# Sums of gate and up weights for a seven-product block multiplication: built in DRAM by accumulating DMAs, or added by VectorE in SBUF

## The chip, the cores and the metric

The kernel runs on one core of one Trainium2 chip. The metric is device time in microseconds, the median of several executions. For the kernel before, three runs gave 2494.14, 2497.13 and 2497.49 us, a median of 2497.13 us.

## What is computed

The reference is one inference step of a two-layer decoder: 1024 prompt tokens and 8 sample tokens with a model width of 1024. Layer 0 mixes by a gated linear recurrence, layer 1 by stick-breaking attention; both add attention over 256 memory tokens and end in a SwiGLU feed-forward network:

```
def swiglu(h, w_gu, w_down):
    gate, up = jnp.split(h @ w_gu, 2, axis=-1)
    return (jax.nn.silu(gate) * up) @ w_down
```

For one layer `w_gu` is 1024 x 5632 (2816 gate columns, then 2816 up columns) and `w_down` is 2816 x 1024, all float32. The change concerns this network of layer 1 for the second half of the tokens, which is the last large stage of the program.

## The kernel before

**Tokens and precision.** The tokens are worked in two groups: group 0 holds 512 prompt tokens, group 1 the other 512 prompt tokens and the 8 sample tokens, so 520 columns. Activations lie with the model dimension on the 128 partitions. Every float32 matrix product is made as three matmuls: each operand is split into a rounded high part and the rest, and high x high, high x low and low x high are accumulated. For weights ScalarE makes the high part (a cast, L260 or L542) and VectorE the low part (a subtraction, L261 or L543).

**The feed-forward network** has 22 blocks of 128 gate columns with their 128 up columns. They are grouped by PARTS (L613) into parts of 5, 5, 4, 4 and 4 blocks. In a part, the blocks give `mids` (silu(gate) x up), and then `w_down` for the same rows is multiplied and added up in `R` (L660 to L676).

**The last network** (class ffn_w, L615, group 1, layer 1) makes blocks 0 to 3 plainly (gate_up_q, L499) and blocks 4 to 21, 18 blocks, by a block multiplication with seven products in place of eight (gate_up_w, L524). The gate weights are cut into upper rows a11 and lower rows a12 (512 rows each), the up weights into a21 and a22, and the tokens into two halves of 260 columns. Seven products `product(ps, 0..6)` (L546) of 12 matmuls each use the weights a11, a21+a22, a11+a21+a22, a12, a11+a21, a11+a21+a22+a12, a22 and matching sums of the activations (sums_w, L326, done once). Between them stand small operations: ScalarE copies one accumulator with a sign change into another ahead of products 2 and 5 (L559, L562), takes silu (L565, L574) and a copy (L568); VectorE adds and subtracts (L570, L572) and multiplies (L575, L576); and the block's result is split for the next product (L281 by ScalarE, L282 by VectorE).

**Where the sums of weights come from.** weight_sums (L588) runs much earlier, in the layer-1 network of group 0 (f1, L1500 to L1503). For each part it makes four DRAM tensors `wsum` of 512 rows by plain and accumulating DMAs that GpSimd issues (L606, L608), eight per part, 40 in all. Each is tied to the progress of f1: ScalarE copies one element of the newest f1 result (`tok`, L602), GpSimd copies that (`mark`, L603), and the DMA is issued behind the mark. In the last network `weight(j)` (L535) then loads each of the seven 512 x 128 weights of a block by one 256 KB DMA on SyncE's queue (L537), three from `w_gu` and four from `wsum`.

**Buffers.** The raw weights come from `wraw` (5 tiles of 128 x 512) and, after the first part, every second one from half a tile of `apool` (8 tiles, of which 4 are kept as `hT`, residual rows for the end, so that 4 remain). `raws` (L630) chooses. The split weights come from `wspl` (5 tiles) and, after the first part, three of eight from `cpool` (4 tiles, one kept by the rows of the sample tokens); `spl` (L624) chooses. `w_down` weights use `wraw` and `wspl` too. `cpool` also carries `yo`, the finished rows of group 0 on their way to DRAM (store_y, L1445, stores L1456): these and the turned residual rows (token_rows, L476, L484) are woven with the first two parts of ffn_w (L1525).

**Order.** Each engine runs its instructions in a fixed order, laid out when the program is built, by a scheduler that sees data dependences and free buffers. All loads of weights and most stores stand in one order on SyncE's queue.

Of the kernel before, what the change touches and what calls it, by code (L numbers as in the profile page):

```python
# [2 lines left out]

# [15 lines left out]
P = 128  # L19
# [5 lines left out]
def tile_decoder(  # L25
# [46 lines left out]
    def nm(s):  # L72
        uid[0] += 1
        return f"{s}_{uid[0]}"
# [12 lines left out]
    def Q(i):  # L87
        return single[0].tile([P, 512], F32, tag=f"q{i}", name=nm("q"))
# [32 lines left out]
    def small(shape, dt=F32, tag="sm", bufs=None):  # L121
        return spool.tile(shape, dt, tag=tag, name=nm(tag), bufs=bufs)
# [105 lines left out]
    def chain(*gens):  # L228
        for g_ in gens:
            yield from g_  # L230
# [92 lines left out]
            out.append(x)  # L323
            yield

    def sums_w(xs, ops):  # L326

        n, h = NG[1], PW[1]  # L330
        for k in range(4):
            x0, x1 = xs[k], xs[k + 4]
            y = YT()
            if k % 2 == 0:
                z, u = YT(), YT()
            o = (k % 2) * h

            def full(x, c):
                t = B()
                nc.vector.tensor_add(t[:, :h], x[:, 0, c : c + h].bitcast(F32), x[:, 1, c : c + h].bitcast(F32))  # L340
# [13 lines left out]
            yield  # L354

    def YT():
        return xpool.tile([P, 2, NG[1]], F32R, tag="x0", name=nm("y"))

    def wo_tiles(g):
# [161 lines left out]
        split_to((mt[:, 0, :n], mt[:, 1, :n]), sg[:, :n])  # L521
        return mt, last

    def gate_up_w(l, f, ops, spl, raws):  # L524

        h, n = PW[1], NG[1]
        part, o = part_of(f)
        gate, up = f * P, DFF + f * P
        src = [
            (w_gu[l][0:512, gate : gate + P], 0), (sums[l][part][0][:, o : o + P], 4), (sums[l][part][1][:, o : o + P], 5),  # L530
            (w_gu[l][512:D, gate : gate + P], 1), (sums[l][part][2][:, o : o + P], 6), (sums[l][part][3][:, o : o + P], 2),
            (w_gu[l][512:D, up : up + P], 3),
        ]

        def weight(j):  # L535
            r = raws()
            nc.sync.dma_start(r, src[j][0].rearrange("(k p) m -> p k m", p=P))  # L537
            return r.rearrange("p k m -> p (k m)")

        def split(src):  # L540
            w = spl()
            nc.scalar.copy(w[:, 0, :], src)  # L542
            nc.vector.tensor_sub(w[:, 1, :], src, w[:, 0, :].bitcast(F32))  # L543
            return w

        def product(ps, j, first=False):  # L546
            w = split(weight(j))
            i = src[j][1]
            for k in range(4):
                x = ops[k][i]  # L550
                for wi, (wj, xi) in enumerate(((0, 0), (0, 1), (1, 0))):
                    nc.tensor.matmul(  # L552
                        ps[:, :h], w[:, wj, k * P : (k + 1) * P], x[:, xi, :],
                        start=(first and k == 0 and wi == 0), stop=(k == 3 and wi == 2), skip_group_check=True,
                    )

        pa, pb, pc, pd = (Q(i) for i in range(4))
        product(pa, 0, True)
        nc.scalar.activation(pb[:, :h], pa[:, :h], AF.Copy, scale=-1.0)  # L559
# [5 lines left out]
        nc.scalar.activation(sg[:, :h], pa[:, :h], AF.Silu)  # L565
        product(pb, 4)
        dt = T()
        nc.scalar.copy(dt[:, h:n], pd[:, :h])  # L568
        gt = T()
        nc.vector.tensor_add(gt[:, h:n], dt[:, h:n], pb[:, :h])  # L570
        product(pc, 5)
        nc.vector.tensor_sub(gt[:, :h], pc[:, :h], dt[:, h:n])  # L572
        product(pb, 6)
        nc.scalar.activation(sg[:, h:n], gt[:, :h], AF.Silu)  # L574
        nc.vector.tensor_mul(sg[:, :h], sg[:, :h], pb[:, :h])  # L575
        nc.vector.tensor_mul(sg[:, h:n], sg[:, h:n], gt[:, h:n])  # L576
        mt = M(F32R)
        split_to((mt[:, 0, :n], mt[:, 1, :n]), sg[:, :n])
        return mt

    sums = {}

    def part_of(f):
        for i, (f0, nf) in enumerate(PARTS):
            if f0 <= f < f0 + nf:
                return i, (f - f0) * P

    def weight_sums(l, parts, after):  # L588

        for i in parts:  # L590
            f0, nf = PARTS[i]
            w = nf * P
            s1, s2, s3, s4 = (tc.dram_tile([512, w], F32, name=nm("wsum")) for _ in range(4))
            sums.setdefault(l, {})[i] = (s1, s2, s3, s4)
            a11, a12 = (w_gu[l][r : r + 512, f0 * P : f0 * P + w] for r in (0, 512))
            a21, a22 = (w_gu[l][r : r + 512, DFF + f0 * P : DFF + f0 * P + w] for r in (0, 512))
            for d, a, add in (
                (s3, a11, False), (s1, a21, False), (s3, a21, True), (s1, a22, True),
                (s2, s3, False), (s2, a22, True), (s4, s2, False), (s4, a12, True),
            ):  # L600
                tok = small([P, 1], tag="rr")
                nc.scalar.copy(tok, after())  # L602
                mark = nc.gpsimd.tensor_copy(small([P, 1], tag="mk", bufs=1), tok)  # L603
                with tc.issue_after(mark.ins):
                    if add:
                        nc.gpsimd.dma_start(d, a, accum_op=ALU.add)  # L606
                    else:
                        nc.gpsimd.dma_start(d, a, max_dma_last_dim=4 * w)  # L608
                yield

    htok = []

# [2 lines left out]
    class ffn_w:  # L615


        def __init__(self, l, x, plain):
            self.g, self.l, self.x, self.ops, self.plain, self.n, self.r, self.pi = 1, l, x, [], plain, 0, 0, 0
            self.R = self.acc = None  # L620
            self.half = []
            self.sums = sums_w(x, self.ops)

        def spl(self):  # L624
            self.n += 1
# [2 lines left out]
            return wspl.tile([P, 2, 512], F32R, tag="ws", name=nm("ws"))  # L628

        def raws(self):  # L630
            self.r += 1
            if self.pi and self.r % 2:
                if not self.half:
                    t = apool.tile([P, 2, 4, P], F32, tag="a", name=nm("w"))
                    self.half = [t[:, 0], t[:, 1]]
                return self.half.pop(0)
            return wraw.tile([P, 4, P], F32, tag="w", name=nm("w"))

        def part(self, pi):
            l, n, h = self.l, NG[1], PW[1]  # L640
# [3 lines left out]
            for j in range(nf):  # L644
                self.pi = pi
                if f0 + j < self.plain:
                    mt, ins = gate_up_q(l, f0 + j, self.x)
                    mids.append(mt)
                    with tc.issue_after(ins.ins):
                        for _ in range((1, 2, 1, 0)[j]):  # L650
                            next(self.sums, None)
                else:
                    mids.append(gate_up_w(l, f0 + j, self.ops, self.spl, self.raws))
                yield
            if pi == 0:
                self.R = R_one()
# [31 lines left out]
    class ffn:  # L688
# [4 lines left out]
        def part(self, pi):  # L693
# [5 lines left out]
            for j in range(nf):  # L699
                pg = proj(g, w_gu[l], 0, ND, (f0 + j) * P, self.xt)  # L700
                sg = silu(None, pg, g)
                pu = proj(g, w_gu[l], 0, ND, DFF + (f0 + j) * P, self.xt)
                nc.vector.tensor_mul(sv(sg, g), sv(sg, g), pv(pu, g))  # L703
                mt = M(F32R)
                split_to((mt[:, 0, :n], mt[:, 1, :n]), sg[:, :n])
                mids.append(mt)
                self.now = sg[:, 0:1]
                yield
            if pi == 0:
                self.R = R_one()  # L710
# [2 lines left out]
            for m in range(ND):  # L713
                ps = proj(g, w_down[l], f0, nf, m * P, mids)
                evac_raw(g, self.R, ps, m, self.acc, pi == 0, last)
                self.now = self.R[m][:, 0:1]
# [842 lines left out]
```

## Time and profile before

| | |
|---|---|
| median of three runs | 2497.13 us |
| profiled execution, its own time | 2499.1 us |
| span of the profiled execution | 2497.4 us |
| TensorE matmul / weight load busy | 2462.8 / 2169.9 us |
| VectorE / ScalarE / GpSimd busy | 1571.8 / 1183.0 / 98.3 us |
| DMA traffic | 358.21 MB, of this 54.53 MB from GpSimd's queue |
| f1 with weight_sums (first to last DMA of weight_sums) | 1036.7 to 1457.0 us |
| ffn_w: plain blocks, block 4, first w_down | from 2115.3, 2164.1, 2176.8 us |
| ffn_w: blocks 5-9, 10-13, 14-17, 18-21 | from 2209.3, 2288.4, 2351.8, 2415.2 us |
| last w_down ends, rows stored | 2481.2, to 2497.4 us |

Times in the profile are counted from the start of the span. A row of grouped instructions gives the line, the engine, the operation, the tile that is written and the tiles that are read, the number of instructions, the busy time and the mean duration of one, and then the idle time of the engine just before them with what ended it. "PE" is TensorE, "PEld" its weight load, "DVE" VectorE, "ACT" ScalarE, "POOL" GpSimd, "SPq" SyncE's DMA queue.

### The profile page before, as it was taken

To read this page: it belongs to the slowest core of one execution; us is meant where nothing else is said; L and a number is where in the kernel's file an instruction comes from. 1 tells how busy PE (TensorE), PEld (TensorE's weight loads), DVE (VectorE), ACT (ScalarE), POOL (GpSimd) and SP (SyncE) were. 2 spreads that over 40 slices of the span, in tenths; PEclk is the share of its full clock that TensorE was granted. 3 is DMA by queue.
4 is the path that set the end of the run, shared out by engine and by line. 5 is a ranking of instruction groups with operands and counts; after the bars stand their busy time and mean duration, and the time that the engine had idled before them with its cause. 6 is when DMAs were issued, how large, how long until landed. Compare 5 with 4: busy or idle time off the path is not lost.

```text
span 2497.4 us, 40764 instructions
## 1 busy us (share of the span) xinstructions
PE 2462.8 (99%) x15565; PEld 2169.9 (87%) x15565; DVE 1571.8 (63%) x2756; ACT 1183.0 (47%) x2277; POOL 98.3 (4%) x139
## 2 busy tenths in 40 slices
PE   8999999999999999999999999999999999999998
PEld 6888988877877897999999989877787797999997
DVE  5766556655765585655544575777577648755655
ACT  5446543243433454555433454555444445564444
POOL 1000000000000000010111100022000000000000
PEclk9999999999999999999999999999999999999999
DMA  5352252233643447586678976544454234365542
GB/s 186 114 165 68 72 156 81 60 110 116 184 124 98 129 138 227 156 195 177 173 191 215 234 193 196 160 142 138 121 149 130 85 115 122 121 192 145 151 137 69
DMA packets 496110, 358.21 MB, mean 143 GB/s; under 512 B 19110, under 2 KB 443635, under 8 KB 495915
## 3 DMA queue, kind: packets, MB, share of 16 engines
q1 hardware_dynamic: 477354, 301.08, 40.5%
q0 software_dynamic: 18560, 54.53, 9.1%
q8 instruction: 122, 2.00, 0.3%
q14 instruction: 74, 0.60, 0.1%
HBM read 325.73 MB, written 75.94 MB: 161 GB/s over the span
## 4 chain that ended last, share of the span: by engine, by line
PE 88%; DVE 5%; DMA 3%; ACT 2%; issue 2%; POOL 0%; SPq 0%; DVEq 0%; ACTq 0%; POOLq 0%
PE mm L274 59%; PE q L552 7%; PE q L667 5%; PE s L1180 2%; PE q L510 2%; PE mm L1048 2%; PE s L903 1%; PE s L862 1%; PE mm L812 1%; DMA b<-qd 1%; PE mm L839 1%; DVE ws L261 1%; PE ns L957 1%; PE s L1336 1%; DMA c<-in_cache_sb_v,pidx 1%
## 5 line engine op out<-in xcount | busy, mean ns | idle before, releaser
L274 PE MATMUL mm<-x,ws 128*128 128x260 f32 (+1 forms) x7776 | 1332.9, 330 | 0.0
L274 PEld LDWEIGHTS mm<-x,ws 128*128 128x128 f32 x7776 | 1148.3, 188 | 151.5 <-issue 12.0
L260 ACT CAST ws<-w 128x512 fp32r<-128x512 f32 x712 | 420.2, 591 | 763.2 <-PE mm L274 620.2
L261 DVE TENSOR_TENSOR ws<-w,ws 128x512 fp32r<-128x512 f32 x712 | 462.5, 653 | 286.8 <-ACT ws L260 278.3
L274 PE MATMUL mm<-m,ws 128*128 128x512 f32 (+1 forms) x2112 | 393.5, 343 | 0.1
L274 PEld LDWEIGHTS mm<-m,ws 128*128 128x128 f32 x2112 | 324.4, 189 | 49.9 <-issue 2.6
L667 PE MATMUL q<-m,ws 128*128 128x260 f32 x1056 | 128.8, 283 | 0.0
L667 PEld LDWEIGHTS q<-m,ws 128*128 128x128 f32 x1056 | 127.2, 188 | 0.4 <-ACT hT L485 0.2
L543 DVE TENSOR_TENSOR ws<-w,ws 128x512 fp32r<-128x512 f32 x126 | 86.6, 691 | 61.5 <-ACT ws L542 59.3
L552 PE MATMUL q<-y,ws 128*128 128x260 f32 x864 | 112.9, 283 | 0.0
L542 ACT CAST ws<-w 128x512 fp32r<-128x512 f32 x126 | 78.0, 621 | 69.6 <-PE q L667 27.4
L552 PEld LDWEIGHTS q<-y,ws 128*128 128x128 f32 x864 | 107.6, 189 | 0.0
L291 DVE TENSOR_SCALAR t<-mm 128x512 f32<-128x512 f32 (+1 forms) x82 | 56.7, 692 | 79.6 <-PE mm L274 79.6
L447 DVE TENSOR_TENSOR r<-r,mm 128x512 f32<-128x512 f32 (+1 forms) x96 | 66.0, 688 | 61.1 <-PE mm L274 60.3
L703 DVE TENSOR_TENSOR t<-t,mm 128x512 f32<-128x512 f32 (+1 forms) x66 | 45.5, 690 | 74.2 <-PE mm L274 73.9
L295 DVE TENSOR_TENSOR t<-t,t 128x512 f32<-128x512 f32 (+1 forms) x66 | 45.8, 694 | 70.6 <-ACT t L294 70.6
L552 PE MATMUL q<-x,ws 128*128 128x260 f32 x648 | 86.3, 282 | 0.0
L552 PEld LDWEIGHTS q<-x,ws 128*128 128x128 f32 x648 | 81.3, 188 | 0.0
L314 DVE TENSOR_TENSOR st<-st,n 128x512 f32<-128x512 f32 (+1 forms) x98 | 67.1, 691 | 8.8 <-ACT n L313 7.0
L281 ACT CAST m<-t 128x512 fp32r<-128x512 f32 (+1 forms) x88 | 54.9, 624 | 18.1 <-DVE t L703 8.9
L282 DVE TENSOR_TENSOR m<-t,m 128x512 fp32r<-128x512 f32 (+1 forms) x88 | 61.0, 693 | 2.6 <-ACT m L281 1.4
L984 POOL DMA_INDIRECT c<-in_cache_sb_k,pidx x16 | 16.4, 1026 | 1170.5 <-ACT n L313 958.6
(339 smaller groups left out, 2557.9 us busy)
## 6 DMA issues: line engine op xcount, KB each, us to landing
w<-in_w_gu SPq DMA_DIRECT2D x334, 256.0 KB, 3.4
w<-in_w_down SPq DMA_DIRECT2D x160, 256.0 KB, 3.5
w<-in_w_in_a SPq DMA_DIRECT2D x80, 256.0 KB, 3.0
wsum<-in_w_gu POOLq DMA_DIRECT2D x18, 1024.0 KB, 9.5
w<-wsum SPq DMA_DIRECT2D x72, 256.0 KB, 3.8
w<-in_w_o SPq DMA_DIRECT2D x64, 256.0 KB, 2.8
wsum<-in_w_gu POOLq DMA_DIRECT2D x12, 1280.0 KB, 10.7
w<-in_w_mem_kv SPq DMA_DIRECT2D x32, 256.0 KB, 3.2
```

The costliest lines, as they stand in the source:

```text
L260: nc.scalar.copy(ws[:, 0, :n, :], raw[:, :n, :])
L261: nc.vector.tensor_sub(ws[:, 1, :n, :], raw[:, :n, :], ws[:, 0, :n, :].bitcast(F32))
L274: nc.tensor.matmul(ps[:, a, : PW[g]], wt, xt[k][:, xi, o : o + PW[g]], start=(k == 0 and wi == 0), stop=(k == nk - 1 and wi == 2),)
L281: nc.scalar.copy(dst[0], src)
L282: nc.vector.tensor_sub(dst[1], src, dst[0].bitcast(F32))
L291: nc.vector.tensor_scalar(sv(x, g), pv(ps, g), -44.0, None, op0=ALU.max)
L314: nc.vector.tensor_add(acc[:, :n], acc[:, :n], t[:, :n])
L447: nc.vector.tensor_add(dst, dst, pv(ps, g))
L542: nc.scalar.copy(w[:, 0, :], src)
L543: nc.vector.tensor_sub(w[:, 1, :], src, w[:, 0, :].bitcast(F32))
L552: nc.tensor.matmul(ps[:, :h], w[:, wj, k * P : (k + 1) * P], x[:, xi, :], start=(first and k == 0 and wi == 0), stop=(k == 3 and wi == 2), ...
L667: nc.tensor.matmul(pp[a][:, :h], wt, mids[k][:, xi, a * h : (a + 1) * h], start=(k == 0 and wi == 0), stop=(k == nf - 1 and wi == 2),)
```

## The change

weight_sums, part_of and the `tok` and `mark` copies go; f1's last three parts run alone. gate_up_w now takes its weights from sums_here: it loads the gate column of the block whole (1024 rows x 128, one DMA of 512 KB) and the up column likewise, into two tiles, and makes the four sums by four VectorE additions (a21+a22; a11+a21; that + a22; that + a12) into `wraw` tiles. a11, a12 and a22 are read where they lie. The two column tiles come from `cpool` for block 4 (first part) and from `apool` afterwards. The seven products, their split and the operations between them are unchanged. Built, the changed program has 72 more VectorE instructions, 40 fewer on ScalarE, 80 fewer on GpSimd and 90 fewer on SyncE, and as many matmuls as before.

```
-    def gate_up_w(l, f, ops, spl, raws):
+    def sums_here(l, f, raws, outs):
+        cols = []
+        for m0 in (f * P, DFF + f * P):
+            r = raws()
+            nc.sync.dma_start(
+                r.rearrange("p a (k m) -> p (a k) m", m=P), w_gu[l][:, m0 : m0 + P].rearrange("(k p) m -> p k m", p=P)
+            )
+            cols.append(r)
+        (a11, a12), (a21, a22) = ((r[:, 0, :], r[:, 1, :]) for r in cols)
+        kept = {}
+
+        def add(a, b):
+            t = outs()
+            nc.vector.tensor_add(t, a, b)
+            return t
+
+        def weight(j):
+            if j == 1:
+                return add(a21, a22)
+            if j == 2:
+                kept[3] = add(a11, a21)
+                kept[2] = add(kept[3], a22)
+                return kept[2]
+            if j == 4:
+                return kept[3]
+            if j == 5:
+                return add(kept[2], a12)
+            return (a11, None, None, a12, None, None, a22)[j]
+
+        return weight
+
+    def gate_up_w(weight, ops, spl, quads):
...
-        def weight(j):
-            r = raws()
-            nc.sync.dma_start(r, src[j][0].rearrange("(k p) m -> p k m", p=P))
-            return r.rearrange("p k m -> p (k m)")
...
-    def weight_sums(l, parts, after):
...
         def raws(self):
-            self.r += 1
-            if self.pi and self.r % 2:
-                if not self.half:
-                    t = apool.tile([P, 2, 4, P], F32, tag="a", name=nm("w"))
-                    self.half = [t[:, 0], t[:, 1]]
-                return self.half.pop(0)
-            return wraw.tile([P, 4, P], F32, tag="w", name=nm("w"))
+            if self.pi:
+                return apool.tile([P, 2, 512], F32, tag="a", name=nm("w"))
+            return C()
...
-    ws = weight_sums(1, range(5), lambda: f1.now)
-    weave((chain(b0.sb(), b0.mem()), 24), (chain(f1.part(0), f1.part(1)), 18), (islice(ws, 16), 17))
-    weave((chain(f1.part(2), f1.part(3), f1.part(4)), 24), (ws, 24))
+    weave((chain(b0.sb(), b0.mem()), 24), (chain(f1.part(0), f1.part(1)), 18))
+    drain(f1.part(2), f1.part(3), f1.part(4))
```

More of the change, by code (lines that the diff above doesn't have):

```diff
@@ L1 @@
 from contextlib import ExitStack
-from itertools import islice
 import concourse.bass as bass
@@ L522, in gate_up_q @@
         return mt, last
-    def gate_up_w(l, f, ops, spl, raws):
-        h, n = PW[1], NG[1]
[L527 to L533, printed above, removed]
-        def weight(j):
-            r = raws()
-            nc.sync.dma_start(r, src[j][0].rearrange("(k p) m -> p k m", p=P))
-            return r.rearrange("p k m -> p (k m)")
+    def sums_here(l, f, raws, outs):
[26 more added lines that the diff above has]
+    def gate_up_w(weight, ops, spl, quads):
+        h, n = PW[1], NG[1]
+        src = (0, 4, 5, 1, 6, 2, 3)
         def split(src):
@@ L555, in product @@
                     )
-        pa, pb, pc, pd = (Q(i) for i in range(4))
+        pa, pb, pc, pd = quads()
         product(pa, 0, True)
@@ L578, in gate_up_w @@
         split_to((mt[:, 0, :n], mt[:, 1, :n]), sg[:, :n])
[L579 to L586, printed above, removed]
-    def weight_sums(l, parts, after):
[L590 to L609, printed above, removed]
+        return mt, last
     htok = []
@@ L652, in part @@
                 else:
-                    mids.append(gate_up_w(l, f0 + j, self.ops, self.spl, self.raws))
+                    mids.append(gate_up_w(
+                        sums_here(l, f0 + j, self.raws, lambda: wraw.tile([P, 512], F32, tag="w", name=nm("w"))),
+                        self.ops, self.spl, lambda: [Q(i) for i in range(4)]
+                    )[0])
                 yield
```

15 lines of the change are left out of this document (6 added, 9 removed).

## Prediction

> **What bounds the kernel now.** I read the page's busy times first, then TensorE's waits in the two stages that the change touches, then the chain of waits of the last stage.
>
> ```profile
> PE 2462.8 (99%) x15565; PEld 2169.9 (87%) x15565; DVE 1571.8 (63%) x2756; ACT 1183.0 (47%) x2277; POOL 98.3 (4%) x139
> ```
> ```profile
> PE s L1363 <- DVE b L1357: 1.6, 4, 0.5
> PE ns L303 <- DVE st L314: 1.2, 1, 1.2
> ```
> ```profile
> 2162.36 1.75 PE q L1451 x16
> 2164.11 10.09 PE q L552 x84
> ...
> 2209.31 50.43 PE q L552 x420
> ```
>
> TensorE is busy for 99% of the span. The second fence is all that it waited between 1030 and 1480 us, where the sums are made in DRAM: 2.8 us. The third is the chain in the last stage: only TensorE, block after block. 420 matmuls in 50.43 us are five blocks of 10.09 us, or 1.44 us a product. So nothing can be won beyond a few microseconds; the question is whether the new feed of weights keeps up with 1.44 us a product.
>
> **Step 1, what goes at 1036 to 1457 us.**
>
> ```profile
> L606 POOL DMA_DIRECT2D wsum<-in_w_gu x20: 998/1028/1097, 1061.5 to 1457.0; - x20
> ```
> ```profile
> 1471.51 0.62 ACT L260 CAST ws<-w 128x512 fp32r<-128x512 f32 x1 [1.99 <-DMA w<-in_w_o]
> ...
> 1478.89 1.13 PE L303 MATMUL ns<-st,ones 128*128 128x512 f32 x2 [1.22 <-DVE st L314]
> ```
>
> Forty DMAs (20 accumulating and 20 plain), 40 one-element copies on ScalarE and 40 marks on GpSimd go. The gain can be no more than TensorE's 2.8 us of waits there. The 1.2 us wait follows a cast that waited for a `w_o` load just after the last accumulating DMA; I count it as won. The four waits on L1357 end a chain of exponentials and a scan beside which the one-element copies are small; I count none. **-1.2 us**, bounds -2.8 and 0.
>
> By the Trainium skill, "DMA: Bandwidth & Descriptors", section "Issuing engines are not separate DMA queues", GpSimd's transfers share the 16 DMA engines with SyncE's, so 54.5 MB less should speed the loads beside them. The trace agrees only in that late `w_o` load; by the rule alone the result would be the gain of the first rival below.
>
> **Step 2, block 4, the first with sums.** Before, its seven weights are loaded while the plain blocks still run, and its sums need no engine. In the built order of the changed kernel, SyncE's queue holds the gate column, then two `yo` stores, and only then the up column. A store can't issue before the rows are turned and copied.
>
> ```profile
> 2147.74 1.65 SPq L537 DMA_DIRECT2D w<-wsum  x2
> ...
> 2164.45 1.94 SPq L1456 DMA_DIRECT2D out_y_prompt<-c  x2
> ```
> ```profile
> w<-in_w_gu SPq DMA_DIRECT2D x334, 256.0 KB, 3.4
> ...
> c<-in_cache_mem_k SPq DMA_DIRECT2D x16, 512.0 KB, 3.9
> ...
> w<-in_w_down SPq DMA_DIRECT2D x64, 64.0 KB, 2.3
> ...
> a<-vsc SPq DMA_DIRECT2D x4, 512.0 KB, 5.5
> ```
> ```profile
> 2288.36 0.76 DVE L676 TENSOR_TENSOR r<-r,q 128x260 f32<-128x260 f32 x2 [1.62 <-PE q L667]
> 2289.04 1.28 DVE L543 TENSOR_TENSOR ws<-w,ws 128x512 fp32r<-128x512 f32 x2
> ```
>
> The first row is a sum's load 16 us ahead of its use. The stores issue until 2166.4 (2164.45 + 1.94), so the up column issues then. No row shows a 512 KB load in the 512-byte pieces of a weight column. 512 KB loads took 3.9 to 5.5 us; weight loads grew by 1.1 us from 64 to 256 KB, so 256 KB more cost some 1.5 or 1.6, and 3.4 + 1.6 gives **5.0 us**, which I take (an estimate; it lies between the two). It lands at 2171.4. A 512-wide VectorE operation takes 0.69 us, and 0.61 from one start to the next (two in 1.28); a 260-wide one 0.42, and 0.34. VectorE's order has three additions ahead of the first low part: 3 x 0.61 + 0.69 = 2.5, so the low part of product 1's weight is there at 2173.9. TensorE would need it after 16 transposes (2164.11), product 0 (1.44), 16 more transposes that the build moves ahead of product 1's third matmul (1.75) and two matmuls (0.24): 2167.5. **+6.4 us**, with other work of block 4 hidden behind it (each later product needs 1.2 us of VectorE or less against 1.44). Bounds: a store issued a microsecond sooner and a 3.9 us load, 4.3; a 5.5 us load with 1.5 us (the growth per 256 KB) for store bytes ahead of it, 8.4.
>
> **Step 3, TensorE's clock after that stop.**
>
> ```profile
> 1883.02 0.63 PE L1363 MATMUL s<-ident,b 128*128 128x128 f32 x4 [2.13 <-DVE b L1357]
> ```
> ```profile
> 1880.00:1890.00 10.00, 7.87 (x31) 6.01 (x30) 8.18 (x11) 3.16 (x6) 0.00 (x0) 0.83 0.35 114
> ```
>
> After an idle 2.13 us the granted clock (third column from the right) was 0.83 over these 10 us, so 0.17 x 10 = 1.7 us of full speed were lost. A stop of 6.4 us should do the same once: **+1.7 us**, bounds 0 and 3.4 (twice).
>
> **Step 4, blocks 5 to 21.** VectorE has these per block, and gets four additions more:
>
> ```profile
> L543 DVE TENSOR_TENSOR ws<-w,ws 128x512 fp32r<-128x512 f32 x113 | 77.8, 691 | 52.2 <-ACT ws L542 50.1 <-DMA w<-in_w_down 1.1
> ...
> L261 DVE TENSOR_TENSOR ws<-w,ws 128x512 fp32r<-128x512 f32 (+1 forms) x37 | 22.3, 605 | 23.6 <-ACT ws L260 23.0
> L260 ACT CAST ws<-w 128x512 fp32r<-128x512 f32 (+1 forms) x37 | 20.4, 552 | 27.3 <-PE q L667 16.4 <-PE q L552 9.1 <-issue 1.8
> L676 DVE TENSOR_TENSOR r<-r,q 128x260 f32<-128x260 f32 x48 | 18.2, 422 | 18.4 <-PE q L667 18.4
> L282 DVE TENSOR_TENSOR m<-t,m 128x520 fp32r<-128x520 f32 x16 | 11.2, 699 | 0.7 <-ACT m L281 0.7
> L281 ACT CAST m<-t 128x520 fp32r<-128x520 f32 x16 | 10.0, 628 | 1.1 <-DVE t L575 1.1
> L572 DVE TENSOR_TENSOR t<-q,t 128x260 f32<-128x260 f32 x17 | 7.3, 428 | 1.8 <-PE q L552 1.6
> L570 DVE TENSOR_TENSOR t<-t,q 128x260 f32<-128x260 f32 x17 | 7.1, 418 | 0.0
> L574 ACT ACTIVATE t<-t 128x260 f32<-128x260 f32 x17 | 7.1, 418 | 2.9 <-DVE t L572 2.9
> L576 DVE TENSOR_TENSOR t<-t,t 128x260 f32<-128x260 f32 x16 | 6.8, 423 | 1.0 <-ACT t L574 1.0
> L575 DVE TENSOR_TENSOR t<-t,q 128x260 f32<-128x260 f32 x16 | 6.7, 419 | 0.2
> L565 ACT ACTIVATE t<-q 128x260 f32<-128x260 f32 x17 | 6.6, 388 | 11.0 <-PE q L552 11.0
> L559 ACT ACTIVATE q<-q 128x260 f32<-128x260 f32 x17 | 6.3, 372 | 5.4 <-PE q L552 5.4
> ```
>
> Eleven operations of 0.61, four of 0.34 and one of 0.62 are 8.7 us of 10.09: it fits, and the splits stand a block ahead of TensorE. What is tight is a loop through the loads. Four `apool` tiles hold the columns of two blocks, and the additions for block b+2 stand in VectorE's order among the splits of b+1. The up column of b+2 can load only when the last split of b has read that tile. Then come the load (5.0), its addition, five splits and additions, L570, a split, an addition, L572 and the next last split: 9 x 0.61 + 2 x 0.34 = 6.2. The loop takes 11.2 us against TensorE's 10.09, so VectorE falls 1.1 us behind per turn. Its lead over the products hides that, but ScalarE's queue doesn't: the copy L559, which product 2 needs 2.88 us into a block, stands behind silu L574 and cast L281 of the block before, and both wait for VectorE. The last split of a block goes out when product 5 of the block before, eight products earlier, has freed its buffer: 8.64 + 0.62 + 0.69, and I allow 0.3 for the handover, is 0.2 into the next block. The column lands at 5.2, L572 starts 5.8 later and ends at 11.4; silu (0.42), a cast of weights (0.62, as in the row of the `w_o` load), the cast L281 (0.63) and L559 (0.37) end at 13.4, which is 3.3 into the next block: 0.4 late. So 0.4 at the first late column of each of the four parts, and 1.1 for each of two more turns in the five-block part: 4 x 0.4 + 2 x 1.1 = **+3.8 us**. Bounds: at a 3.9 us load the loop takes 10.1, so 0; with the gate column queued ahead (5.0 + 1.6) it takes 12.8, so 4 x 2.0 + 2 x 2.7 = 13.4.
>
> At the end of a part, an addition may stand ahead of the last L282; the 18 matmuls of the earlier `mids` (2.2 us) cover it. Without that cover it would cost 0.6 a part.
>
> **Sum.** -1.2 + 6.4 + 1.7 + 3.8 = +10.7 us. The profiled execution took 2499.1 us (span 2497.4 and 1.7 around it), so 2509.8 in its terms; it lies 2.0 above the median of 2497.1, and the same difference on the median gives **2507.8 us**.
>
> **The rivals.**
>
> *The feed is in time, and the freed DMA engines show.* The up column of block 4 would have to land by 2165.0 (2167.5 - 2.5), so issue by 2160.0, before the stores' rows are turned at 2162.4. If SyncE doesn't hold it behind the stores, steps 2 and 3 vanish; with loads under 4 us step 4 does too, and only step 1 is left, at most -2.8: 2494.3 us. For it speaks that the loads shrink from 1.75 to 1 MB a block; against it, the fixed order of the queue. Chance 0.10.
>
> *VectorE becomes the bound throughout.* If it keeps its present waits for ScalarE, then from 2209 to 2455 us its busy 157 us (the VectorE rows above), 68 additions of 0.69 (47) and waits of 76 (52.2 + 23.6) are 280 us in a window of 246: +34, and with steps 1 to 3 +41: 2538 us. For it: each split still follows a cast. Against: those waits are now slack that TensorE's pace leaves. Chance 0.13.
>
> *Block 4 stalls, the rest hides.* -1.2 + 6.4 + 1.7 = +6.9: 2504.0. This lies inside the forecast's range.
>
> **How the numbers follow.** Forecast with its third variant 0.70, first rival 0.10, second 0.13, something else 0.07 (counted as slower). The ends are the sums of the bounds: -2.8 + 4.3 + 0 + 0 = +1.5, 2498.6; and 0 + 8.4 + 3.4 + 13.4 = +25.2, 2522.3. They leave out the two rivals, some 2 in 10. 0.2% is 5.0 us, about what a measurement of this kernel can tell from no change: faster is below 2492.1, slower above 2502.1. The first rival gives 0.05 faster and 0.05 the same, the forecast's low end 0.08 more the same; slower 0.82.
>
> **What will show it.** Right: TensorE idle 4 to 8 us once in block 4, ended by VectorE's split, with an addition waiting for a `w_gu` load and a lower granted clock after it; VectorE's additions waiting for loads in blocks 7 to 9 and in later parts, and TensorE idle under 2 us behind L559's successor there; nothing over 3 us won before 2030 us. Wrong: TensorE full through block 4 (step 2); idle in most blocks behind VectorE's splits (second rival); a shorter stretch from 1036 to 1480 by more than 3 us (step 1).

## The result and the profile after

The changed kernel took **2506.32 us** (median of 6 runs, 2505.61 to 2509.66), the kernel before 2497.31 us beside it (6 runs, 2494.14 to 2500.11): a ratio of 1.0041, with a 95% interval of 1.0028 to 1.0054. It is slower by some 9 us. The profiled execution took 2508.42 us with a span of 2506.7 us, against 2499.1 and 2497.4.

On the page of the changed kernel, TensorE's line reads much as before: nearly full, with 6.6 us more of busy time for the same 15565 matmuls. The next thing to read is therefore where these matmuls ran slower or later.

```profile
PE 2469.4 (99%) x15565; PEld 2173.6 (87%) x15565; DVE 1612.5 (64%) x2828; ACT 1179.7 (47%) x2237; POOL 47.4 (2%) x59
```

**Block 4.** The chain of waits of the changed kernel between 2155 and 2185 us (start, duration, what) leaves TensorE, goes through ScalarE's copies and a store's issue to the load of the up column, then through one addition and a cast back to TensorE. Before, the same stretch was TensorE alone.

```profile
2163.83 0.60 ACT c L1439
2164.42 0.53 ACT ws L561
2164.95 0.21 SPq L1441
2165.16 0.05 issue
2165.22 6.27 DMA c<-in_w_gu
2171.49 0.02 issue
2171.51 0.70 DVE w L536
2172.21 0.02 issue
2172.24 0.63 ACT ws L561
2172.86 0.04 issue
2172.91 0.80 PE q L571 x2
```

The timeline of the same stretch shows the order on SyncE's queue (SPq) that the prediction read from the build: gate column, two `yo` stores, up column. It also shows a stop that the prediction did not have: product 0 waits 1.38 us for its first cast, which stands on ScalarE behind the copies for these stores although the gate column was issued 28 us earlier.

```profile
2135.77 0.50 SPq L527 DMA_DIRECT2D c<-in_w_gu  x1
...
2163.54 1.62 SPq L1441 DMA_DIRECT2D out_y_prompt<-c  x2
2164.30 0.64 ACT L561 CAST ws<-c 128x512 fp32r<-128x512 f32 x1
...
2164.99 0.51 PE L571 MATMUL q<-x,ws 128*128 128x260 f32 x2 [1.38 <-ACT ws L561]
2165.22 0.46 SPq L527 DMA_DIRECT2D c<-in_w_gu  x1
...
2171.51 0.69 DVE L536 TENSOR_TENSOR w<-c 128x512 f32<-128x512 f32 x1 [5.84 <-DMA c<-in_w_gu]
...
2174.21 2.08 PE L571 MATMUL q<-y,ws 128*128 128x260 f32 x8
```

In windows cut finely (third column from the right: granted clock) TensorE is at half clock from within the second window below to within the last: 2 x 0.33 us are lost in the second, 8 x 0.50 us in the windows between, up to 2176, and 2 x 0.23 us in the last. That makes 5.1 us, which is 10.2 us at half clock.

```profile
2163.60:2165.00 1.40, 0.02 (x2) 0.01 (x1) 0.61 (x2) 1.34 (x3) 0.00 (x0) 1.00 0.48 184
...
2166.00:2168.00 2.00, 2.00 (x13) 1.74 (x12) 0.00 (x0) 0.37 (x1) 0.00 (x0) 0.67 0.99 273
...
2176.00:2178.00 2.00, 2.00 (x15) 2.00 (x14) 1.68 (x3) 1.12 (x2) 0.00 (x0) 0.77 0.54 157
```

**Blocks 5 to 21.** All that TensorE waited for in the changed kernel from 2150 us on (us in total, times, longest) is six rows; two are the end of the program (L754, L738). The fourth row, L571 behind VectorE's L589, is the one in the later parts; the other three are block 4.

```profile
PE q L571 <- ACT ws L561: 2.5, 2, 1.4
PE q L754 <- DVE yT L758: 2.3, 1, 2.3
PE q L738 <- DVE st L313: 1.5, 1, 1.5
PE q L571 <- DVE t L589: 1.4, 2, 1.3
PE q L483 <- ACT c L1439: 0.7, 1, 0.7
PE q L1436 <- ACT c L1439: 0.7, 1, 0.7
```

**Where the 9.3 us of span went.** Executions differ by up to 4.5 us before the last network begins (its first matmul starts between 2111.7 and 2116.2 us, whatever was changed), but from there on a stretch of TensorE in which nothing is late repeats to 0.1 us, and the tail to 0.3. Block 4 with its stop repeats less well: 101.82 to 102.50 us in the five kernels that have it unchanged (after, E3, E4, E6, E7). So the table takes, from the timeline of TensorE, the time from the first matmul of one stage to the first of the next; the tail runs from the last `w_down` matmul's end to the end of the span. It holds all experiments, told below; the last column is the ratio of their times to those of the kernel before on the same chip. One of E8's twelve runs took 3011.95 us at a granted clock of 0.75 and is left out; all other runs were at 0.99 or above.

| kernel | plain blocks to block 5 | blocks 5-9 | 10-13 | 14-17 | w_down after 17 | 18-21 | tail | ratio [95%] |
|---|---|---|---|---|---|---|---|---|
| before | 93.81 | 50.44 | 40.34 | 40.37 | 23.03 | 40.36 | 16.06 | |
| after | 102.45 | 50.49 | 41.88 | 40.82 | 23.35 | 40.38 | 14.86 | 1.0041 [1.0028, 1.0054] |
| E1 both columns of block 4 early | 93.79 | 50.46 | 40.37 | 40.89 | 23.35 | 40.38 | 14.91 | 1.0003 [0.9994, 1.0012] |
| E4 before, block 4 alone changed | 102.30 | 50.43 | 40.34 | 40.37 | 23.03 | 40.36 | 16.33 | 1.0037 [1.0024, 1.0051] |
| E9 only its up column early | 96.54 | 50.46 | 41.49 | 40.75 | 23.35 | 40.38 | 14.92 | 1.0017 [1.0008, 1.0026] |
| E5 TensorE kept busy | 100.97 | 50.47 | 40.37 | 41.07 | 23.34 | 40.38 | 14.89 | 1.0031 [1.0021, 1.0042] |
| E7 more column buffers | 101.82 | 50.46 | 40.37 | 40.36 | 23.35 | 40.38 | 14.83 | 1.0033 [1.0020, 1.0046] |
| E8 both repairs (E1 + E7) | 93.79 | 50.46 | 40.37 | 40.36 | 23.35 | 40.38 | 14.82 | 0.9996 [0.9987, 1.0005] |
| E10 E8, 6 additions a block | 93.76 | 50.46 | 40.37 | 40.37 | 23.23 | 40.38 | 15.02 | 0.9999 [0.9990, 1.0008] |
| E11 E8, 8 additions a block | 93.78 | 51.11 | 40.37 | 40.37 | 23.22 | 40.38 | 14.88 | 1.0001 [0.9992, 1.0010] |
| E6 additions on GpSimd | 101.97 | 53.63 | 41.68 | 42.29 | 26.70 | 40.65 | 14.95 | 1.0064 [1.0051, 1.0077] |
| E3 after, the forty DMAs kept | 102.50 | 50.81 | 41.64 | 40.90 | 23.32 | 40.40 | 14.94 | 1.0042 [1.0029, 1.0055] |
| E2 before, other token buffers | 93.80 | 50.52 | 40.39 | 40.43 | 23.03 | 40.40 | 14.89 | 0.9995 [0.9986, 1.0004] |

From before to after: block 4 costs 8.64 us, blocks 5 to 21 and the `w_down` after block 17 cost 0.05 + 1.54 + 0.45 + 0.32 + 0.02 = 2.4, the tail gives back 1.20, and the last network began 0.5 us earlier: +9.3.

### The profile page after: what moved, and what is told of

The parts are those of the page before. It is cut to its first block, busy times and chain, and to the rows that moved or that the text cites. A ratio compares the mean times of both kernels' runs of the same rounds, so it can differ in the third digit from the quotient of the medians.

```text
span 2506.7 us, 40415 instructions
## 1 busy us (share of the span) xinstructions
PE 2469.4 (99%) x15565; PEld 2173.6 (87%) x15565; DVE 1612.5 (64%) x2828; ACT 1179.7 (47%) x2237; POOL 47.4 (2%) x59
## 2 busy tenths in 40 slices
DMA packets 451018, 297.88 MB, mean 119 GB/s; under 512 B 17029, under 2 KB 413906, under 8 KB 450826
## 4 chain that ended last, share of the span: by engine, by line
PE 90%; DVE 5%; DMA 2%; ACT 2%; issue 1%; SPq 0%; POOL 0%; DVEq 0%; ACTq 0%
PE mm L273 61%; PE q L571 7%; PE q L654 5%; PE s L1165 2%; PE q L509 2%; PE mm L1033 2%; PE s L888 1%; PE s L847 1%; PE mm L797 1%; PE mm L824 1%; PE ns L942 1%; PE s L1321 1%; DMA b<-qd 1%; PE s L1360 1%; DVE ws L260 1%
## 5 line engine op out<-in xcount | busy, mean ns | idle before, releaser
L571 PE MATMUL q<-y,ws 128*128 128x260 f32 x864 | 114.6, 285 | 2.5 <-DVE t L589 1.4
L571 PEld LDWEIGHTS q<-y,ws 128*128 128x128 f32 x864 | 108.7, 191 | 3.4 <-DVE t L589 1.9
L571 PE MATMUL q<-x,ws 128*128 128x260 f32 x648 | 87.4, 284 | 1.5 <-ACT ws L561 1.4
L571 PEld LDWEIGHTS q<-x,ws 128*128 128x128 f32 x648 | 82.0, 189 | 2.0 <-ACT ws L561 1.6
L280 ACT CAST m<-t 128x512 fp32r<-128x512 f32 (+1 forms) x88 | 54.9, 624 | 21.8 <-DVE t L690 9.0
L291 ACT ACTIVATE t<-t 128x512 f32<-128x512 f32 (+1 forms) x66 | 42.0, 636 | 33.3 <-DVE t L290 28.4
```

The source lines that it names most:

```text
L280: nc.scalar.copy(dst[0], src)
L571: nc.tensor.matmul(ps[:, :h], w[:, wj, k * P : (k + 1) * P], x[:, xi, :], start=(first and k == 0 and wi == 0), stop=(k == 3 and wi == 2), ...
```

## The experiments

**Theory** after the result: block 4 stops because its up column is issued behind two stores, the half clock adds to it, and the later parts lose by the loop through the column buffers. **Rivals**: the additions themselves, that is VectorE, are the bound; what is freed on the DMA engines is worth something that hides in the sum; and for the tail, chance.

### Block 4: E1, E4, E9

E1 loads both columns before plain block 2:

```
+                if pi == 0 and j == 2:
+                    early = columns(l, self.plain, self.raws)
...
+    sums_here(columns(l, f0 + j, self.raws) if pi else early, ...)
```

> The changed kernel, with both column loads of block 4 written ahead of plain block 2, so that they issue some 40 us before their use and stand ahead of the stores in SyncE's queue; nothing else is moved by hand. Theory (the up column issued too late, behind the two stores, and the half clock that followed): block 4 loses nothing, the first part's w_down starts within 0.5 us of 2176.8 less 0.5, so some 8.5 us are won back: 2497.8 us, and no waiting of VectorE's additions for a load before 2215 us. Rival A (the additions themselves are the price, VectorE is the bound in block 4): no more than the 1.4 us of the first cast come back: 2505. Rival B (only the order of SyncE matters, the cast behind ScalarE's copies stays late): 2499.5.

Measured: 93.79 us to block 5 against 93.81 before; 2498.78 us (11 runs) against 2497.74 of the kernel before. The additions stayed on VectorE, and all of the 8.64 us came back, so Rival A is out for block 4. The time missed the theory's 2497.8 by 1.0 us; it can't be told from the kernel before. Two additions before 2215 us still waited for a load, 2.3 us in all, which the theory had at none; TensorE didn't wait for them. In E1's chain of waits the stretch is TensorE alone again, sixteen transposes and then seven products without a stop:

```profile
2160.10 1.75 PE q L1441 x16
2161.85 10.09 PE q L574 x84
```

Rival B can't be judged by E1, since in its build the first casts moved ahead of the copies together with the loads; E9 below parts the two.

E4 puts only block 4 of the change into the kernel before (the other blocks' sums still come from DRAM):

```
+    here = None if pi else sums_here(l, f0 + j, C, ...)
+    mids.append(gate_up_w(l, f0 + j, self.ops, self.spl, self.raws, here))
```

> The kernel before, with block 4 alone changed: its two columns are loaded whole and VectorE adds; blocks 5 to 21 keep the sums from DRAM, and all forty DMAs that make sums stay. Theory: the stall of block 4 alone, +8.6 us: 2505.9, with TensorE's granted clock at 0.50 for some 10 us from 2167 us on. Rival (the price in block 4 comes from the other blocks' changed loads, or from freed DMA engines): under +3 us.

Measured: 102.30 us to block 5, +8.49, and 2506.41 us: nearly the whole loss of the change by one block of 18. The half clock was shorter than expected: in the windows from 2160 to 2184 us it is 0.72 over 6 us, 3.4 us at half clock, and follows the long stop.

```profile
2166.00:2172.00 6.00, 2.23 (x16) 1.52 (x15) 1.20 (x2) 1.96 (x4) 0.00 (x0) 1.00 0.59 165
2172.00:2178.00 6.00, 5.68 (x33) 5.29 (x34) 5.09 (x9) 4.29 (x10) 0.00 (x0) 0.72 0.22 66
```

E9 loads only the up column early (the first line runs at `j == 2`); the gate column's load and its cast stay where they were:

```
+    up = columns(l, self.plain, self.raws, (1,))
...
+    sums_here(columns(l, f0 + j, self.raws, (0, 1)) if pi else
+              columns(l, f0 + j, self.raws, (0,)) + up, ...)
```

> The changed kernel, with only the up column of block 4 loaded ahead of plain block 2; the gate column keeps its place, and in the built order its first cast still stands behind the copies for the stores in ScalarE's queue. It parts the two delays of block 4: the late column and the late first cast. Theory (the column is the one that decides; the cast's stop of 1.4 us was hidden in front of it, and is what is late next): one stop of 1.4 us in block 4, and the stretch from the plain blocks to the first part's w_down takes 62.6 us, against 61.2 in the kernel before and 69.9 in the changed one; 3.1 us longer than 61.2 if a stop of 1.4 us alone brings the half clock. Rival (the late cast is the main cause): 66 us or more.

Measured: 96.54 us to block 5, +2.73 (64.0 us to the first part's w_down, by the expectation's measure); 5.9 of the 8.64 us were the up column's, with the half clock that follows its stop. What was late next was the first cast, with the same stop of 1.38 us, and a short one behind it. TensorE's waits in block 4 of E9:

```profile
PE q L575 <- ACT ws L565: 1.4, 1, 1.4
PE q L575 <- ACT q L582: 0.4, 1, 0.4
```

That is 0.9 us more than these two stops; the granted clock stayed at 1.00, so it isn't the clock, as the expectation's 3.1 us had it. By the starts of TensorE's matmuls all of it lies ahead of product 3: product 0 starts 3.29 us after the transposes' start where it was 1.67 before, and from there product 3 starts after 5.51 us where it was 4.41, together 2.72 us. So the late first cast and the gaps in the products just behind it are all that is left. The main cause is the column; the cast alone was worth less than a third.

### The clock: E5

E5 gives TensorE 52 matmuls of no use during the stop:

```
+        filler(fill[0])          # n = 12
         product(pa, 0, True)
+        filler(fill[1])          # n = 40
```

> The changed kernel, with 52 idle matmuls of 260 columns added in block 4 (12 ahead of product 0, 40 ahead of product 1), into a bank that product 1 then starts afresh: TensorE has 6.2 us of work while it waits for the first cast and for the up column. Outputs are the same. Theory (the stall's length is set by the column; half clock costs only what of it lies behind the column's arrival, 2.7 us at 0.50 from 2174.2 to 2176.9): clock 1.00 throughout, the part's w_down starts 1.4 us earlier than in the changed kernel, at 2183.6 us, time 2504.9. Rival A (all of the 10 us of half clock are paid for): some 4 us less, 2502.3. Rival B (the clock follows the load on TensorE over a longer time and falls anyway): 2506 to 2510.

Measured: 100.97 us to block 5, 1.48 less than the changed kernel. The windows show a granted clock of 1.00 throughout:

```profile
2164.00:2174.00 10.00, 9.72 (x81) 9.35 (x80) 3.80 (x6) 3.12 (x7) 0.00 (x0) 1.00 0.49 159
2174.00:2184.00 10.00, 10.00 (x85) 9.86 (x84) 7.82 (x16) 7.38 (x17) 0.00 (x0) 1.00 0.70 220
```

The 1.48 us aren't the clock's alone. In E5 the column landed 5.1 us after its issue instead of 6.3, but its cast then stood behind a copy for a store on ScalarE, and product 1's third matmul started 59.15 us after the network's first, against 59.37 in the changed kernel. From that matmul to the first `w_down` E5 took 9.26 us, the changed kernel 10.50, and the four others with the same block 4 (E3, E4, E6, E7) 10.1 to 11.3. So the half clock behind the column's arrival cost some 1.2 us, 0.9 to 2.0 over the five kernels; of the 10.2 us at half clock the rest was not paid for, because TensorE was waiting for the column anyway. The whole time, 2505.14 us, doesn't tell 1.5 us from none; the stretch does.

### Blocks 5 to 21: E7, E8, E10, E11

E7 puts the up columns into `bpool`'s half-column buffers, idle in this stage, so that `apool`'s four tiles hold gate columns alone:

```
+            if m0 >= DFF and up:
+                r = [up(), up()]
...
+                                  B if pi else None),
```

> The changed kernel, with the up columns of blocks 5 to 21 in another group of seven half-column buffers that is idle in this stage (each up column then comes as two loads of half the size), so that the four whole-column buffers hold gate columns alone and a column can be loaded a block earlier. Theory (step 4: a loop through the loads, since a column can only be loaded when the block two before it has read its last split): no addition waits for a load after 2217 us, and the parts take 50.4, 40.4, 40.4 and 40.4 us: 2504.0. Rival (VectorE's own work, not the loads, makes the parts longer): parts 2 and 3 stay 1.5 and 0.5 us longer, 2506.

Measured: 50.46, 40.37, 40.36 and 40.38 us, and from block 5's start on no addition waited for a load. The parts lost nothing. The up columns also come as halves now, but it is the buffers that decide: by the built order the last half of block 13's up column is the one issued at 2285.37 us, 22.6 us ahead of its addition, where the changed kernel has 5.7, the whole landing time of its load. Only the 0.32 us in the `w_down` after block 17 stayed; it is there in every kernel with VectorE's additions from block 5 on, but for E10 and E11 with 0.2. The time, 2506.35 us, still has block 4's stop in it, and 2 us are less than it can tell.

What a late column does is seen in blocks 10 to 13. The chain of waits of the changed kernel goes from VectorE's last split of a block into the up column's load, 5.69 us, then along VectorE's queue to the subtraction-and-add L589, for which TensorE's next product waits 1.26 us:

```profile
2306.83 5.69 DMA w<-in_w_gu
...
2315.64 0.60 DVE ws L562
2316.25 0.34 DVE t L589
2316.59 0.04 issue
2316.64 3.38 PE q L571 x26
```

In E1, whose loop is the changed kernel's, the same load was issued at the same point of the part (10.35 us after its first matmul) and took 3.8 us; the part lost 0.03 us. From E1's timeline:

```profile
2296.41 0.37 SPq L527 DMA_DIRECT2D w<-in_w_gu  x1
...
2300.24 0.69 DVE L539 TENSOR_TENSOR w<-w 128x512 f32<-128x512 f32 x1 [0.84 <-DMA w<-in_w_gu]
```

The addition for which that load is made waited much longer in the changed kernel:

```profile
2312.55 0.69 DVE L536 TENSOR_TENSOR w<-w 128x512 f32<-128x512 f32 x1 [2.73 <-DMA w<-in_w_gu]
```

By the same reading the load took 3.8 us in E5 (the addition waited 0.78 us, 0.03 lost), 5.4 in E3 (2.46 waited, 1.30 lost) and 5.3 in E9 (2.32 waited, 1.15 lost). So the loss follows the landing time of one DMA. In the three kernels that lose, the wait is 1.2 us more than the loss (2.73 less 1.54, 2.46 less 1.30, 2.32 less 1.15): that is VectorE's lead over TensorE at this point. Why the landing time differs from kernel to kernel wasn't found.

E8 joins both repairs.

> The changed kernel with both repairs: block 4's columns loaded ahead of plain block 2, and the up columns of blocks 5 to 21 in the group of half-column buffers. Theory: all that the change cost is gone, and what it won stays (1.2 us in the tail, some 0.5 at 1036 to 1457 us): 1.7 us less than the kernel before, 2496.0, with TensorE waiting only in the tail after 2116 us. Rival (something else in the change costs time that the two repairs don't touch): 2498 or more.

Measured: every stretch as before but for 0.32 us, and the tail shorter: from the first matmul of the last network to the end of the span 381.2 us against 382.1. The time was 2497.07 us (median of 11) against 2497.89, a ratio of 0.9996 [0.9987, 1.0005]: no difference that can be told. Of the expected 1.7 us, 1.2 are in the tail; the 0.5 at 1036 to 1457 us are not to be found (E3 below).

E10 and E11 test how near VectorE is to being the bound, by making two or all four additions of a block twice in E8:

```
             nc.vector.tensor_add(t, a, b)
+            if next(again):
+                nc.vector.tensor_add(t, a, b)
```

> The kernel with both repairs, with two of the four additions of each of blocks 5 to 21 made twice (same operands, same result, the second overwrites the first). It adds 2 x 0.61 us to VectorE's 8.7 us a block, 9.9 of 10.09. Theory (VectorE's waits are slack that TensorE's pace leaves): nothing is lost, the blocks of the parts take 50.4, 40.4, 40.4 and 40.4 us, the time is that of the kernel with both repairs, 2497.3. Rival (the waits for ScalarE's casts are not slack, VectorE is near the bound with four additions already): 34 x 0.61 = 21 us more of VectorE's time, most of it lost, 2512 or more.

> The kernel with both repairs, with all four additions of each of blocks 5 to 21 made twice. VectorE then has 8.7 + 4 x 0.61 = 11.1 us a block against TensorE's 10.09. Theory: VectorE becomes the bound at about this point; it falls 1.0 us behind per block, the first 1.4 us of each part are hidden by a product, so the parts lose about 3.8, 2.7, 2.7 and 2.7 us: 12 us in all, 2509. Rival A (a longer lead hides it): 2498. Rival B (VectorE's waits come on top): over 20 us, 2518 or more.

Measured: E10's blocks lost nothing, E11's 0.65 us in the five-block part and nothing in the others; 2496.99 and 2498.03 us. The expectation of 12 us for E11 was wrong, and Rival A there right: VectorE's lead at the start of a part hides more than one product. Four blocks at 1.0 us each were hidden, and of five all but 0.65; at 11.13 us of work a block against 10.09 the lead must have been at least some 4.5 us (5 x 1.04 - 0.65, an estimate; VectorE still stood idle for 6.1 of the 51 us below). This holds for E8's buffers, in which columns are loaded early. The first windows of E8 and then of E11 show VectorE's busy time (fourth figure) in the five-block part:

```profile
2206.00:2257.00 51.00, 51.00 (x427) 51.00 (x426) 38.01 (x69) 30.41 (x65) 0.00 (x0) 1.00 0.41 118
```
```profile
2206.00:2257.00 51.00, 50.63 (x421) 50.42 (x421) 44.94 (x83) 29.42 (x63) 0.00 (x0) 1.00 0.42 121
```

### GpSimd instead of VectorE: E6

```
-            nc.vector.tensor_add(t, a, b)
+            eng.tensor_add(t, a, b)        # nc.gpsimd from block 5 on
```

> The changed kernel, with the additions of blocks 5 to 21 on GpSimd instead of VectorE; block 4 is left as it is. Theory (in parts 2 and 3 VectorE's queue stands still at an addition that waits for the up column, and TensorE then waits for what is queued behind it): the blocks of the parts take 50.4, 40.4, 40.4 and 40.4 us, 2.3 us less than in the changed kernel: 2504.0. Rival A (GpSimd takes longer for an addition than a product takes, 1.44 us, or slows VectorE beside it): the blocks take over 10.5 us each, +10 us or more: 2516 or above. Rival B (the losses in the parts come from the loads themselves, whoever adds): unchanged, 2506.

Measured: 2514.65 us, and every part is longer. The theory's forecast failed, for a reason of the other engine: an addition takes GpSimd 1.37 to 1.54 us in the mean, against 0.69 on VectorE, and VectorE's splits rose from 0.69 us to 0.96 in the mean. The groups of GpSimd, and of VectorE from 2218 us on, in E6:

```profile
L536 POOL TENSOR_TENSOR w<-w,w 128x512 f32<-128x512 f32 x51 | 78.6, 1542 | 33.5 <-DVE ws L562 18.3 <-DVE ws L260 8.6 <-issue 5.0
L536 POOL TENSOR_TENSOR w<-w 128x512 f32<-128x512 f32 x17 | 23.4, 1374 | 576.8 <-DMA w<-in_w_gu 490.8 <-DVE ws L260 72.5 <-DVE ws L562 13.3
```
```profile
L562 DVE TENSOR_TENSOR ws<-w,ws 128x512 fp32r<-128x512 f32 x116 | 110.1, 963 | 31.0 <-ACT ws L561 29.6
```

In the timeline a split beside a GpSimd addition took 1.76 us, alone 0.68. Which of the two costs the time, the long additions or the slowed splits, E6 doesn't part. Rival A came nearest: the blocks of the four parts took 10.7, 10.4, 10.6 and 10.2 us each (the stretches by 5, 4, 4, 4), and the `w_down` after block 17 lost 3.7 us. E6 says nothing for or against the loop.

### The early stage and the tail: E3, E2

E3 puts the forty DMAs back, unused (`ws = weight_sums(...)` and its place in the weave, tokens in buffers of their own).

> The changed kernel, with the forty DMAs that make sums in DRAM put back between 1036 and 1457 us; their results are not used by anything, so this adds work and changes no output. The tokens are in a buffer group of their own, so that the tail stays as in the changed kernel. It measures step 1 by itself. Theory (TensorE hardly waits there, with or without them): TensorE's wait of 1.2 us behind a late w_o load comes back, all else stays: +0.5 to +1.2 us against the changed kernel, 2507.2. Rival (what is freed on the DMA engines is worth more, and hides in the changed kernel's gains): +3 us or more, spread over the stretch from 1036 to 1480 us.

Measured: 2507.88 us, a ratio of 1.0042 where the changed kernel has 1.0041. TensorE's wait behind the `w_o` load did not come back. All that it waited from 1030 to 1480 us in E3, with all the DMAs running:

```profile
PE s L1381 <- DVE b L1375: 1.6, 4, 0.5
```

It is absent in E4 too, which also keeps them, and present in E2 (1.1 us). So neither theory nor rival came true: the transfers of the forty DMAs (344.04 MB move in E3, 297.88 in the changed kernel) are worth nothing that these runs can show, with ratios of 1.0042 and 1.0041 whose intervals are 0.0013 either way.

E2 asks where the tail's 1.2 us come from. In the built order of ScalarE the two kernels differ in one wait at the end:

```
before: L756 LoadActFuncSet [waits PE_49]
        L756 Activation rr_25032<-q_25026,epsb 128x4 [waits Pool_49]
after:  L741 LoadActFuncSet
        L741 Activation rr_24805<-q_24799,epsb 128x4 [waits PE_49]
```

The removed tokens were `rr` tiles, read last by GpSimd, and the last part's first `rr` tile takes such a buffer: its instruction had two things to wait for, and the wait for TensorE was put on the table load ahead of it.

```
-                tok = small([P, 1], tag="rr")
+                tok = small([P, 1], tag="tk")
```

> The kernel before, with one word changed: the one-element tokens that GpSimd reads are drawn from a buffer group of their own instead of the one that the last part's rr tiles use. Theory (in the kernel before, the last part's first rr tile waits for GpSimd's old read besides TensorE, so that TensorE's wait is put ahead of ScalarE's table load, which then runs alone): the table load starts beside TensorE's last sums, as in the changed kernel, and the stretch after the last w_down matmul is 1.2 to 1.3 us shorter; the time is 1.2 us less, 2496.1, and all else is as before. Rival (the 1.2 us in the tail came from less DMA or from chance): the table load starts after TensorE's last sum as before, no change.

Measured: the tail took 14.89 us against 16.06, and the table load starts with TensorE's sums instead of after them. The timelines of the kernel before and then of E2:

```profile
2484.46 0.20 PE L754 MATMUL q<-ones,st 128*8 128x1 f32 x2
2484.74 1.28 ACT L756 ACT_TABLE_LOAD   x1 [1.29 <-PE q L754]
```
```profile
2482.14 1.28 ACT L756 ACT_TABLE_LOAD   x1
...
2483.34 0.20 PE L754 MATMUL q<-ones,st 128*8 128x1 f32 x2
```

The time, 2496.58 us against 2497.74, is in the right direction and not beyond its interval; the stretch shows it.

## Why the prediction was right or wrong

The forecast was 2507.8 us, measured 2506.3: slower and inside the range. The two terms of block 4, steps 2 and 3, were right in mechanism and within 0.8 us; step 4 had the right cause but another path and size, step 1 was not confirmed, and one term was missing. That the sum came within 1.5 us is partly luck. Block 4 cost 0.5 us more than steps 2 and 3 together and the parts 1.4 less than step 4; of step 1's 1.2 us at most the 0.5 by which the last network began earlier is seen, and the tail gave 1.2 us that nobody forecast. These partly cancel.

**Step 1 (-1.2).** Not confirmed. The one wait that I took for the DMAs' doing is gone in the changed kernel, but E3 and E4 have all forty DMAs and not the wait. The step's bounds (-2.8 to 0) held, its value rested on one execution's late load. The Trainium skill's rule quoted there ("DMA: Bandwidth & Descriptors", section "Issuing engines are not separate DMA queues") may well hold, but here the shared engines were not what TensorE waited for: of the 450 us from 1030 to 1480, TensorE was busy 448.3 us with the forty DMAs (E3) and 448.4 without (the changed kernel).

**Step 2 (+6.4).** Right in place and mechanism, by E1, E4 and E9. Product 1 went on at 2174.21 us where 2167.0 was needed (2167.5, less the 0.5 us by which the network began earlier): +7.2. The column was issued at 2165.2, as the order of the queue said (2165.9 by the working, less the same 0.5), but took 6.3 us and not the 5.0 of my estimate; that is within the bound, which allowed for the stores' bytes ahead of it. The chain of additions took 2.7 us from landing to matmul, where 2.5 were worked out. Missed was the late first cast; it hid in front of the column and shows only when the column is repaired. The sign of being right looked different too: TensorE wasn't idle once for 4 to 8 us, ended by VectorE's split, but four times for 3.9 us in all, ended by ScalarE each time, with transposes at half clock between.

**Step 3 (+1.7).** Right: some 1.2 us by E5. But the record of the clock looked different, 10.2 us at half rather than 3.4, and only E5 showed how little of it counts. The Trainium skill, "TensorE: Matmul & The Clock Gate", Part 1, says that the clock is decided in free-running windows of 3.4 us. The trace agrees as far as it goes: 10.2 us is three of them, E4's 3.4 us is one, and the same stop of 1.38 us was soon followed by half clock in the changed kernel and by none in E9.

**Step 4 (+3.8).** The loop was the cause (E7: nothing lost without it), its size 2.4 us and its path wrong. I had the late column reach TensorE through ScalarE's queue, at the copy L559 of the next block, and 2.6 us lost in the five-block part. It reached TensorE through VectorE's own queue, at L589 of the block that TensorE was working (it reads the accumulator that product 6 then adds to), and the five-block part lost 0.05 us although three additions waited there for loads. The wait rows of the changed kernel from 2216 to 2268 us hold no row of TensorE, and this:

```profile
DVE w L536 <- DMA w<-in_w_gu: 3.3, 3, 1.6
```

VectorE's lead covers them, at most 1.6 us at a time; in blocks 10 to 13 it covered 1.2 of 2.73 us. The working has a slip as well: by its own list L572 starts 8 x 0.61 + 0.34 = 5.2 us behind the landing, not 5.8 (2317.71 less 2312.55 in the trace of the changed kernel). With 5.2 the first late column of a part costs nothing through L559, and the step comes to some 2.1 us, all of it in the five-block part, where 0.05 was lost. So the 2.4 us that were measured don't confirm the working; that the size is near is luck. With a load of 3.8 us the loss is nothing, as the lower bound said; with 5.3 to 5.7 us it is 1.2 to 1.5 in one part. The end of a part, which I put at 0, costs 0.3 once: after block 17 a cast for the next part's weights waits 1.59 us for an addition and stands ahead of the last cast L280, for which TensorE's weight load then waits 0.25 us. That was only read from the timeline of the changed kernel, not tested:

```profile
2401.69 0.62 ACT L561 CAST ws<-w 128x512 fp32r<-128x512 f32 x1 [1.59 <-DVE w L536]
...
2404.10 0.62 ACT L280 CAST m<-t 128x520 fp32r<-128x520 f32 x1
```

**Missing:** the tail's -1.2 us. It could have been read from the built order; the prediction compared the stages that the change names and not the waits of the untouched end.

**Rivals.** *The feed is in time* was wrong as the kernel stands, and its condition was the right one: with the column early (E1, E8) steps 2 and 3 vanish. Its gain is not there: E8 took 2497.07 us, where this rival had 2494.3. *VectorE becomes the bound* is refuted: twice the additions cost 0.65 us in the blocks of all the parts (E11). *Block 4 stalls, the rest hides* (2504.0) had block 4 right; the rest lost 2.4 us.

## What to carry to other kernels

Where a load is made larger and fewer, look first at the place in the DMA queue that the first one gets: what is issued behind a store waits for the computation that feeds the store, and here one column of 512 KB in the wrong place cost 5.9 of the 9.3 us. A stop of TensorE should be priced by what arrives last, and the half clock only behind that arrival. And removing an instruction can remove a wait elsewhere: compare the waits of the whole built order, down to code that the diff doesn't touch.

## What the hardware showed unexpectedly

- The same 512 KB column load, at the same place of the loop, landed after 3.8 us in two kernels and after 5.3 to 5.7 us in three; in block 4, issued right behind two stores, it took 5.1 (E5) to 6.3 us (the changed kernel).
- GpSimd's additions slowed VectorE's splits from 0.69 to 0.96 us in the mean (E6), and a single one to 1.76 us.
- A stop of TensorE of 1.38 us was followed by half clock from 1.7 us after its end in one kernel, and by none in E9 with the same stop.
